# Two of the four sums of weight blocks of a pair made by accumulating transfers of GpSimd's queue

## The chip, the cores and the metric

The kernel runs on one core of a Trainium2 chip. The metric is the device time of one execution in microseconds (us). The profile names the engines PE (TensorE), DVE (VectorE), ACT (ScalarE), POOL (GpSimd) and SP (SyncE, which here issues most loads and stores).

## The reference

One inference step of a two-layer decoder of width 1024 in float32, for a prompt of 512 positions and 8 samples of 8 positions, together 576 columns. Layer 0 is a gated short convolution, layer 1 an mLSTM block with matrix memory:

```python
# layer 0
b_gate, c_gate, xa, z = split(h @ w_in, 4)          # 1024 -> 4 x 2048
conv = causal_dwconv(c_gate * xa, buf, conv_w)
out  = (b_gate * conv * silu(z)) @ w_out            # 2048 -> 1024
# layer 1
xm, z = split(h @ w_in, 2)                          # 1024 -> 2 x 2048
xc = silu(causal_dwconv(xm, conv_buf, conv_w) + conv_b)
q, k, v = xc @ w_q, xc @ w_k, xm @ w_v              # 2048 -> 2048 each
...
hh, C, n, m = mlstm_chunkwise(q, k, v, gates, C0, n0, m0)
out = ((layernorm(hh) * onorm_w) + skip * xc) * silu(z) @ w_out
```

Each layer begins with an RMS norm and ends with a residual add; a last norm follows.

## The kernel before, in words

Activations lie in SBUF as tiles of 128 channels x 576 columns. A chunk of weights is 512 KB: 128 partitions x 8 blocks of 128 x 128, that is 1024 inputs for 128 outputs. To keep float32 accuracy every product is made of three matmuls: both operands are split into a high part (cast to fp32r on ScalarE, `wh`, L250 or L202) and the rest (VectorE, `wl`, L251 or L203). There are four buffers each for `wh` and `wl`.

In 38 places two chunks are worked on as a pair, by a Strassen-like scheme (`block_pair`): the pair's weights are four blocks a11, a12 (of the tile r1) and a21, a22 (of r2), and seven products of 12 matmuls (128 x 288 columns) take the place of eight. The products, in order, are p6 with s2, p1 with a11, p5 with s1, then a12, a21, a22 and again s2. For them four sums of blocks are made on VectorE, each 128 x 512:

- s1 = a21 + a22 (L286) and s2 = s1 + a11 (L287), in `block_weights`, called ahead of the pair;
- a21 + a11, in place (L327), and s2 + a12, in place (L328), in `block_pair`, for the fifth and the seventh product.

The activations' forms (`fa`, `fb`: differences of the halves of two tiles, L257 to L260, with their `hi` and `lo`) are the other operands.

14 pairs are in layer 0 (the c_gate and xa chunks; after each pair two plain chunks for b_gate and z run into `acc`, L222), 8 make the values (v) and 16 the keys and queries of layer 1; there each pair also adds two plain chunks (L368). Layer 1's input projection (`acc`, then `xm`, L628, its short convolution `xc`, L440 and L442) runs just ahead of the value pairs. After a value or a key pair, GpSimd copies the samples' columns (`dup`, `kd`, L671), TensorE transposes them (`ta`, `tb`) and they are stored.

All loads of weights leave from SP's queue, in order. A scheduler sets the order of the instructions on each engine when the program is built, from its own model of the times; on the chip each engine works through its list strictly in order and waits on semaphores where an operand or a buffer isn't ready. So a wait at the head of a list holds all that stands behind it. `weight_tile()` gives one of a few raw weight tiles, `X(...)` a scratch tile of another small pool.

Of the kernel before, what the change touches and what calls it, by code (L numbers as in the profile page):

```python
# [12 lines left out]
ALU = mybir.AluOpType  # L13
# [54 lines left out]
def trunk(tc, io):  # L68
    nc = tc.nc
    ctx = ExitStack()  # L70
    with ctx:
# [32 lines left out]
        def X(n=NT, name="x"):  # L104

            if not layer0[0]:
                return T(n, name=name)
            uid[0] += 1
            return loads[1].tile([P, n], F32, name=f"{name}{uid[0]}", tag="X", bufs=7)
# [13 lines left out]
        def block(name="blk"):  # L123
            uid[0] += 1
            return accs[1].tile([P, 512], F32, name=f"{name}{uid[0]}", tag="blk", bufs=4)[:, 0:HT]
# [12 lines left out]
        load = nc.sync.dma_start  # L138
        store = nc.sync.dma_start
        store_act = nc.scalar.dma_start  # L140

        cols = const.tile([P, NCOL], F32, name="cols")
        cst = const.tile([P, NCST], F32, name="cst")
# [31 lines left out]
        def run(n=1):  # L175
            for _ in range(min(n, len(work))):
                work.popleft()()
# [14 lines left out]
        def weight_tile():  # L192
            return load_tile("wr", "raw").rearrange("p a (k x) -> p (a k) x", x=P)
# [51 lines left out]
        def parts_of(src):  # L245

            uid[0] += 1
            hi = wpool.tile([P, 4, P], F32R, name=f"wh{uid[0]}", tag="hi", bufs=4)
            lo = wpool.tile([P, 4, P], F32R, name=f"wl{uid[0]}", tag="lo", bufs=4)
            last_act[0] = nc.scalar.copy(hi, src).ins  # L250
            nc.vector.tensor_tensor(lo, src, hi.bitcast(F32), ALU.subtract)  # L251
            return hi, lo
# [26 lines left out]
        def block_weights(c1, c2):  # L279

            r1, r2 = weight_tile(), weight_tile()
            for r, c_ in ((r1, c1), (r2, c2)):
                latest[0] = load(out=r, in_=io["wts"][c_]).ins
            a11, a12, a21, a22 = [r[:, i:8:2, :] for r in (r1, r2) for i in range(2)]
            s1, s2 = [X(512, name="ws").rearrange("p (k x) -> p k x", x=P) for _ in range(2)]
            nc.vector.tensor_tensor(s1, a21, a22, ALU.add)  # L286
            nc.vector.tensor_tensor(s2, s1, a11, ALU.add)  # L287
            ahead_of[c1, c2] = a11, a12, a21, a22, s1, s2

        def block_pair(c1, c2, fs, xs, out1, out2, add, mid=None, then=None, pops=0):  # L290

            a11, a12, a21, a22, s1, s2 = ahead_of.pop((c1, c2))
            o11, o12, o21, o22 = out1[:, 0:HT], out1[:, HT:NT], out2[:, 0:HT], out2[:, HT:NT]
            pu = X(name="pu")
            p, u = pu[:, 0:HT], pu[:, HT:NT]
            tt = nc.vector.tensor_tensor

            def product(bank_, w, form, start):  # L300
                for j in range(4):
                    hi, lo = fs[j][form]
                    for i, (a, x) in enumerate(((w[0], hi), (w[0], lo), (w[1], hi))):
                        nc.tensor.matmul(bank_, a[:, j, :], x, start=(start and j == 0 and i == 0), stop=(j == 3 and i == 2),  # L304
                                         skip_group_check=True)

            b1 = block("p6")
            product(b1, parts_of(s2), "t2", True)
            b0 = block("p1")
            product(b0, parts_of(a11), "b11", True)  # L310
            nc.scalar.copy(p, b0)
            run(pops)
            b2 = block("p5")
            product(b2, parts_of(s1), "t1", True)
            if add:
                tt(o12, o12, b1, ALU.subtract)
                tt(o12, o12, p, ALU.add)
            else:
                tt(o12, p, b1, ALU.subtract)
            run(pops)  # L320
            product(b0, parts_of(a12), "b21", False)
            if add:
                tt(o22, o22, b2, ALU.subtract)
                tt(o22, o22, p, ALU.subtract)
            else:
                tt(o22, p, b2, ALU.add)
            tt(a21, a21, a11, ALU.add)  # L327
            tt(s2, s2, a12, ALU.add)  # L328
            run(pops)
            product(b1, parts_of(a21), "t3", False)  # L330
            run(pops)
            b3 = block("p4")
            product(b3, parts_of(a22), "t4", True)
            tt(u, b1, p, ALU.subtract)
            if add:
                tt(o22, o22, b1, ALU.add)
            else:
                tt(o22, b1, o22, ALU.subtract)
            run(pops)
            product(b2, parts_of(s2), "b22", False)  # L340
            if mid:
                mid()
            if then:
                block_weights(*then)
            if add:
                tt(o11, o11, b0, ALU.add)
                tt(o21, o21, b3, ALU.add)
                tt(o21, o21, u, ALU.add)
            elif xs is None:
                nc.scalar.copy(o11, b0)  # L350
                tt(o21, b3, u, ALU.add)
            else:
                plain(b3, b1, c2 + 1, xs, False)
                tt(o21, b3, u, ALU.add)
                tt(o22, b1, o22, ALU.add)
                plain(b0, b2, c1 + 1, xs, None)
                nc.scalar.copy(o11, b0)
            tt(o12, o12, b2, ALU.add)
# [114 lines left out]
        for k in range(KD):  # L473
# [3 lines left out]
            if k in (0, 3):  # L477
                for c_ in range(2):
                    i = 4 * (k // 3)
# [1017 lines left out]
def _chunks(w):  # L1497
    k, m = w.shape
    return w.reshape(k // D, KD, P, m // P, P).transpose(3, 0, 2, 1, 4)


def _arrays(a):
    f = {n: np.asarray(v) for n, v in a.items()}
    x = np.concatenate([f["x_prompt"].reshape(NP, D), f["x_sample"].reshape(NS, D)], 0)
    win = _chunks(f["a_w_in"][0]).reshape(4, NW, P, KD, P)
    ain = win[[1, 2, 3, 0]].transpose(1, 0, 2, 3, 4)
    bin_ = _chunks(f["b_w_in"][0])
    kq = np.stack([_chunks(f["b_w_k"][0]), _chunks(f["b_w_q"][0])], 1)
    wts = np.concatenate([t.reshape(-1, P, KD, P) for t in (
        ain, _chunks(f["a_w_out"][0]), bin_[:NW], _chunks(f["b_w_v"][0]), kq, bin_[NW:], _chunks(f["b_w_out"][0]))], 0)  # L1510
    cols = np.zeros((P, NCOL), np.float32)

    def put(name, v):
        v = v.reshape(-1, P).T
        cols[:, COLS[name]:COLS[name] + v.shape[1]] = v

    put("norm0", f["norm_w"][0])
    put("norm1", f["norm_w"][1])
    put("fin", f["final_norm_w"])
    for j in range(3):  # L1520
        put(f"ca{j}", f["a_conv_w"][0, j])
    for j in range(4):
        put(f"cb{j}", f["b_conv_w"][0, j])
    put("cbias", f["b_conv_b"][0])
    put("skip", f["b_skip"][0])
    put("onorm", f["b_onorm_w"][0])
    cols[:, COLS["eps"]] = 1e-6

    def ext(st):
        n = st.shape[1]  # L1530
        e = np.zeros((4, P, 4, 8, 8 + n), np.float32)
        e[..., :n] = st.reshape(8, n, 4, 4, P).transpose(2, 4, 3, 0, 1)
        return e.reshape(4, P, -1)

    wif = f["b_w_if"][0].reshape(3, 4, 4, P, 8)[[2, 1, 0]]
    wp = np.zeros((3, 4, P, 4, 32), np.float32)
    wp[..., :8] = wif.transpose(0, 1, 3, 2, 4)
    cst, keep, dmask = _consts()
    g16 = np.zeros((16, 42), np.float32)
    bif = f["b_b_if"][0]  # L1540
    g16[:, 0] = np.repeat(bif[:4], 4)
    g16[:, 1] = np.repeat(bif[4:], 4)
    g16[:, 2:10] = np.repeat(f["state_m"][0].T, 4, 0)
    g16[:, 10:] = dmask
    cs = f["state_C"][0].reshape(2, 4, 4, 4, P, 512).transpose(2, 0, 3, 4, 1, 5)
    ns = f["state_n"][0].reshape(2, 4, 4, 4, P).transpose(4, 2, 0, 3, 1)
    return {
        "xT": x.T.reshape(KD, P, NT), "wts": wts, "cols": cols, "cst": cst, "g16": g16, "keep": keep,
        "exa": ext(f["state_conv_a"][0]), "exb": ext(f["state_conv_b"][0]), "wif": wp.reshape(12, P, P),
        "cs": cs.reshape(32, P, 4, 512), "nst": ns.reshape(P, 128),  # L1550
    }
# [42 lines left out]
```

## Time and profile before

| | us |
|---|---|
| three runs | 1714.5, 1715.65 (median), 1722.03 |
| profiled execution, its time | 1715.56 |
| span in the profile, first to last instruction | 1713.5 |
| TensorE busy | 1669.4 (97%) |
| VectorE busy | 1105.3 (65%) |
| ScalarE busy | 685.3 (40%) |
| GpSimd busy | 107.7 (6%) |

A row of a timeline gives the start, the duration (both us), the engine, the line, the operation, out<-in, the shape, how many, and in brackets how long the engine sat idle before it and what released it. `SPq` and `ACTq` rows are issues of transfers on the queues of SP and ACT; their duration is that of the issue, and where several are put together (x2), from the first to the last. A row of waits gives the engine and operation, what it waited for, the total in us, how often, and the longest. A row of a group ends with its busy time, the mean of one in ns, and the idle time ahead of it.

In the profile the pairs of layer 0 run from 51 us to about 390 us, the value pairs from 612 us, the key/query pairs from 837 to 1271 us. After that come the matrix memory and the output projection, without pairs.

### The profile page before, as it was taken

How to read it: one execution, taken by the hardware profiler on the slowest of the kernel's cores; microseconds unless marked ns; L12 is line 12 of the kernel's file. 1: busy time of each engine (PE TensorE's matmuls, PEld its weight loads, DVE VectorE, ACT ScalarE, POOL GpSimd, SP SyncE). 2: the span in 40 equal slices, each digit the busy share in tenths (PEclk: the TensorE clock that was granted, in tenths of full speed). 3: DMA queues.
4: the chain of work that ended last, by engine and by line, in shares of the span. 5: the costliest groups of instructions: out<-in, count | busy, mean ns of one | idle time of the engine just before them, and what ended most of it. 6: DMA issues, size and time to landing. Idle time of an engine off the chain costs nothing.

```text
span 1713.5 us, 30944 instructions
## 1 busy us (share of the span) xinstructions
PE 1669.4 (97%) x12315; PEld 1591.1 (93%) x12315; DVE 1105.3 (65%) x2078; ACT 685.3 (40%) x1252; POOL 107.7 (6%) x241
## 2 busy tenths in 40 slices
PE   9999999999999999999999999999999998898998
PEld 8999999999999999999999889899899787898898
DVE  6977877774436896555846345355468556778755
ACT  5433343342323553433534233233246455554421
POOL 0000000000000001000110010000021000000000
PEclk9999999999999999999999999999999899999999
DMA  5223322223432434434423552642745588797973
GB/s 193 74 83 99 103 86 85 90 73 137 141 115 87 141 122 151 138 111 154 152 88 120 188 178 87 219 154 62 271 161 195 201 280 286 247 361 249 362 276 105
DMA packets 107487, 275.23 MB, mean 161 GB/s; under 512 B 11056, under 2 KB 33456, under 8 KB 107344
## 3 DMA queue, kind: packets, MB, share of 16 engines
q1 hardware_dynamic: 91984, 255.95, 45.0%
q10 hardware_dynamic: 15360, 17.32, 2.9%
q8 instruction: 97, 1.59, 0.4%
q14 instruction: 46, 0.38, 0.1%
HBM read 211.13 MB, written 62.09 MB: 159 GB/s over the span
## 4 chain that ended last, share of the span: by engine, by line
PE 88%; DMA 5%; DVE 4%; ACT 2%; issue 1%; SPq 0%; POOL 0%; DVEq 0%; ACTq 0%; POOLq 0%
PE acc L222 34%; PE p L304 24%; PE p L368 16%; DMA c<-cs 2%; PE qa L759 2%; PE r L1122 2%; DMA cs_out<-c 1%; DMA wr<-wts 1%; PE g L661 1%; PE num L1175 1%; PE ta L680 1%; PE cp L1175 1%; PE num L1176 1%; PE s L778 1%; PE blk L368 1%
## 5 line engine op out<-in xcount | busy, mean ns | idle before, releaser
L222 PE MATMUL acc<-hi,wh 128*128 128x256 f32 (+1 forms) x1520 | 331.7, 299 | 11.1 <-ACT z L875 6.8
L222 PE MATMUL acc<-hi,wl 128*128 128x256 f32 (+1 forms) x1520 | 330.8, 299 | 0.0
L222 PE MATMUL acc<-lo,wh 128*128 128x256 f32 (+1 forms) x1520 | 330.2, 299 | 0.0
L202 ACT CAST wh<-wr 128x512 fp32r<-128x512 f32 x286 | 176.5, 621 | 328.6 <-PE acc L222 174.5
L304 PE MATMUL p<-hi,wh 128*128 128x288 f32 x968 | 286.7, 299 | 3.7 <-ACT wh L250 2.1
L304 PE MATMUL p<-lo,wh 128*128 128x288 f32 x968 | 284.5, 295 | 0.0
L304 PE MATMUL p<-hi,wl 128*128 128x288 f32 x968 | 279.2, 295 | 1.2 <-DVE wl L251 1.2
L222 PEld LDWEIGHTS acc<-hi,wh 128*128 128x128 f32 x1520 | 257.8, 191 | 16.0 <-ACT z L875 7.0
L203 DVE TENSOR_TENSOR wl<-wr,wh 128x512 fp32r<-128x512 f32 x286 | 195.8, 689 | 118.4 <-ACT wh L202 115.8
L222 PEld LDWEIGHTS acc<-hi,wl 128*128 128x128 f32 x1520 | 257.8, 191 | 2.2 <-issue 1.2
L222 PEld LDWEIGHTS acc<-lo,wh 128*128 128x128 f32 x1520 | 257.7, 191 | 0.7 <-issue 0.5
L250 ACT CAST wh<-wr 128x512 fp32r<-128x512 f32 x152 | 94.5, 622 | 258.4 <-PE p L368 116.7
L304 PEld LDWEIGHTS p<-hi,wh 128*128 128x128 f32 x968 | 181.9, 188 | 7.8 <-ACT wh L250 3.7
L304 PEld LDWEIGHTS p<-lo,wh 128*128 128x128 f32 x968 | 182.4, 188 | 0.0
L304 PEld LDWEIGHTS p<-hi,wl 128*128 128x128 f32 x968 | 179.9, 188 | 1.4 <-DVE wl L251 1.4
L368 PE MATMUL p<-hi,wh 128*128 128x288 f32 x736 | 169.9, 299 | 0.0
L368 PE MATMUL p<-lo,wh 128*128 128x288 f32 x736 | 166.9, 294 | 0.0
L368 PE MATMUL p<-hi,wl 128*128 128x288 f32 x736 | 166.4, 296 | 0.2 <-DVE wl L203 0.2
L251 DVE TENSOR_TENSOR wl<-ws,wh 128x512 fp32r<-128x512 f32 x114 | 78.7, 691 | 119.6 <-ACT wh L250 119.4
L250 ACT CAST wh<-ws 128x512 fp32r<-128x512 f32 x114 | 70.8, 621 | 187.8 <-PE p L368 108.3
L251 DVE TENSOR_TENSOR wl<-wr,wh 128x512 fp32r<-128x512 f32 x152 | 104.9, 691 | 52.3 <-ACT wh L250 50.5
L368 PEld LDWEIGHTS p<-hi,wh 128*128 128x128 f32 x736 | 120.8, 188 | 14.7 <-issue 11.2
(371 smaller groups left out, 2557.2 us busy)
## 6 DMA issues: line engine op xcount, KB each, us to landing
wr<-wts SPq DMA_DIRECT2D x222, 512.0 KB, 3.6
c<-cs SPq DMA_DIRECT2D x112, 512.0 KB, 5.8
cs_out<-c SPq DMA_DIRECT2D x64, 512.0 KB, 6.7
x<-xT SPq DMA_DIRECT2D x16, 288.0 KB, 4.1
xcs<-xc ACTq DMA_DIRECT2D x16, 288.0 KB, 2.2
x<-xcs SPq DMA_DIRECT2D x16, 288.0 KB, 4.1
x<-x1s SPq DMA_DIRECT2D x16, 288.0 KB, 4.5
ld<-xcs SPq DMA_DIRECT2D x16, 288.0 KB, 7.5
```

The source lines that it names most:

```text
L202: last_act[0] = nc.scalar.copy(hi, raw[:, 4 * i:4 * i + 4, :]).ins
L203: nc.vector.tensor_tensor(lo, raw[:, 4 * i:4 * i + 4, :], hi.bitcast(F32), ALU.subtract)
L222: nc.tensor.matmul(acc[:, o:o + j - i], a[:, k % 4, :], x[:, i:j], start=(first and k == 0 and p == 0), stop=(last and k == 7 and p == 2))
L250: last_act[0] = nc.scalar.copy(hi, src).ins
L251: nc.vector.tensor_tensor(lo, src, hi.bitcast(F32), ALU.subtract)
L304: nc.tensor.matmul(bank_, a[:, j, :], x, start=(start and j == 0 and i == 0), stop=(j == 3 and i == 2), skip_group_check=True)
L368: nc.tensor.matmul(b, a[:, k % 4, :], x[:, t:t + HT], start=bool(new) and k == 0 and i == 0, stop=(k == 7 and i == 2), skip_group_check=True)
L661: nc.tensor.matmul(g[32 * j:32 * j + 32, 0:b - a], w[:, 32 * j:32 * j + 32], tiles[j][:, a:b], start=True, stop=True)
L680: nc.tensor.transpose(pa[:, 128 * it:128 * it + 128], t[:, 128 * it:128 * it + 128], ident)
L759: nc.tensor.matmul(st["q"][32 * g:32 * g + 32, :], st["qp"][dt // 2][:, dt % 2, 128 * u + 32 * g:128 * u + 32 * g + 32], ct[g // 2][:, g % ...
L1122: nc.tensor.matmul(r, kst[2 * i + j][:, 128 * dt:128 * dt + 128], vst[:, 0:512], start=True, stop=True)
L1175: nc.tensor.matmul(acc[:, 256:512], w, b[:, 0:256], **ends)
```

## The change

s1 and a21 + a11 are no longer made by VectorE. The host lays the blocks of the chunks concerned out so that the blocks of the even inputs come first (a permutation of the eight blocks; a11 is then `r1[:, 0:4]`, a12 `r1[:, 4:8]`). s1's tile is loaded with the first half of chunk c2 from HBM (256 KB, SP), and a transfer of GpSimd's queue with `accum_op` add then adds c2's second half to it. Another such transfer adds c1's first half to a21 in the tile r2. s2 and its second sum stay on VectorE. Line numbers behind move by one to three (L287 becomes L290, L251 becomes L252, L628 L630, L671 L673).

```diff
+        add_load = nc.gpsimd.dma_start
...
             for r, c_ in ((r1, c1), (r2, c2)):
                 latest[0] = load(out=r, in_=io["wts"][c_]).ins
-            a11, a12, a21, a22 = [r[:, i:8:2, :] for r in (r1, r2) for i in range(2)]
+            a11, a12, a21, a22 = [r[:, i:i + 4, :] for r in (r1, r2) for i in (0, 4)]
             s1, s2 = [X(512, name="ws").rearrange("p (k x) -> p k x", x=P) for _ in range(2)]
-            nc.vector.tensor_tensor(s1, a21, a22, ALU.add)
+            load(out=s1, in_=io["wts"][c2][:, 0:4, :])
+            add_load(out=s1, in_=io["wts"][c2][:, 4:8, :], accum_op=ALU.add)
+            add_load(out=a21, in_=io["wts"][c1][:, 0:4, :], accum_op=ALU.add)
             nc.vector.tensor_tensor(s2, s1, a11, ALU.add)
...
-            tt(a21, a21, a11, ALU.add)
             tt(s2, s2, a12, ALU.add)
...
+    blk = [c for c in range(8, 64) if c % 4 < 2] + list(range(96, 192, 2))
+    wts[blk] = wts[blk][:, :, [0, 2, 4, 6, 1, 3, 5, 7]]
```

In the whole program VectorE has 76 instructions fewer, SP 38 loads more, GpSimd 76 transfers more. TensorE's list keeps its instructions and nearly their order. Three places show what else moved.

The first pair of layer 0, on VectorE. The rows give line, operation, out<-in, shape; `wr_644` and `wr_645` are r1 and r2, `ws_648` is s1, `ws_649` s2. Before:

```order
L286 TENSOR_TENSOR ws_648<-wr_645 128x512
L258 TENSOR_TENSOR fa_654<-x_133,fa_654 128x288
L287 TENSOR_TENSOR ws_649<-ws_648,wr_644 128x512
L327 TENSOR_TENSOR wr_645<-wr_645,wr_644 128x4x128
L260 TENSOR_TENSOR fb_655<-x_133,fa_654 128x288
L160 TENSOR_TENSOR lo_661<-fa_654,hi_660 128x576
L251 TENSOR_TENSOR wl_702<-ws_649,wh_701 128x512
```

And now:

```order
L161 TENSOR_TENSOR lo_663<-fa_656,hi_662 128x576
L161 TENSOR_TENSOR lo_667<-fb_657,hi_666 128x576
L544 TENSOR_TENSOR u_504<-raw_306,raw_304 128x576
L439 COPY ext_502<-u_504 128x8x8
L581 TENSOR_TENSOR z_684<-raw_379,rb_464 128x576
L290 TENSOR_TENSOR ws_649<-ws_648,wr_644 128x512
L442 SCALAR_TENSOR_TENSOR cv_505<-u_504,cols,cv_505 128x511
L444 SCALAR_TENSOR_TENSOR cv_505<-ext_502,cols,cv_505 128x64
L442 SCALAR_TENSOR_TENSOR cv_505<-u_504,cols,cv_505 128x510
L252 TENSOR_TENSOR wl_704<-ws_649,wh_703 128x512
```

The s2 sum stands behind the last two `fa` and `fb`, both `lo`, and `u`, `ext` and `z` of the convolution, which came behind the pair's `wl` rows before; on ScalarE the activations `cv` and `z` likewise stand ahead of the cast of s2.

The first value pair, on VectorE and GpSimd. Before, on VectorE (`ws_6840` is s1, `ws_6841` s2):

```order
L286 TENSOR_TENSOR ws_6840<-wr_6837 128x512
L440 SCALAR_TENSOR_TENSOR xc_6823<-xm_6333,cols,xc_6823 128x511
L442 SCALAR_TENSOR_TENSOR xc_6823<-ext_6056,cols,xc_6823 128x64
L287 TENSOR_TENSOR ws_6841<-ws_6840,wr_6836 128x512
L327 TENSOR_TENSOR wr_6837<-wr_6837,wr_6836 128x4x128
```

Now, first on VectorE, then on GpSimd (`ws_6854` is this pair's s1, `ws_6855` its s2; `wr_7161` is r2 of the second pair, `ws_7164` its s1):

```order
L290 TENSOR_TENSOR ws_6855<-ws_6854,wr_6850 128x512
L630 TENSOR_TENSOR xm_6919<-acc_6860,rb_5883 128x576
L439 COPY ext_6693<-xm_6919 128x8x8
L252 TENSOR_TENSOR wl_7040<-ws_6855,wh_7039 128x512
L252 TENSOR_TENSOR wl_7057<-wr_6850,wh_7056 128x512
L330 TENSOR_TENSOR ws_6855<-ws_6855,wr_6850 128x512
L252 TENSOR_TENSOR wl_7075<-ws_6854,wh_7074 128x512
L161 TENSOR_TENSOR lo_6922<-xm_6919,hi_6921 128x576
L630 TENSOR_TENSOR xm_6996<-acc_6937,rb_5883 128x576
```

```order
L289 DMA wr_7161<-wts 128x512
L288 DMA ws_6854<-wts 128x512
L640 COPY cpb<-xm_6919 128x3
L640 COPY cpb<-xm_6996 128x3
L288 DMA ws_7164<-wts 128x512
```

The s2 sum now has the `xm` of the last two input chunks behind it, and on GpSimd the transfer that makes s1 stands behind the second pair's a21. On SP the load into `ws_6854` (L287) stands right behind the loads of the second pair, `wr_7160` and `wr_7161`.

The first two key/query pairs, on SP. Before, with `wr_9859` and `wr_9860` the second pair's r1 and r2:

```order
L283 DMA wr_9859<-wts 128x1024
L283 DMA wr_9860<-wts 128x1024
L171 DMA x_9373<-xcs 128x576
L171 DMA x_9375<-xcs 128x576
```

And now, with `ws_9424` s1 of the first pair, `ws_9886` that of the second, `wr_10034` r1 of the third:

```order
L284 DMA wr_9882<-wts 128x1024
L284 DMA wr_9883<-wts 128x1024
L172 DMA x_9395<-xcs 128x576
L172 DMA x_9397<-xcs 128x576
L287 DMA ws_9424<-wts 128x512
L689 DMA vss_7026<-tb_9461 256x1x128
L689 DMA vss_7026<-tb_9487 256x1x128
L689 DMA vss_7026<-tb_9624 256x1x128
L689 DMA vss_7026<-tb_9650 256x1x128
L284 DMA wr_10034<-wts 128x1024
L287 DMA ws_9886<-wts 128x512
```

The loads into s1 stand behind the last `x` loads and behind the third pair's r1. In the steady rows of layer 0 the load of s1 stands between r1 and r2 of the same pair.

## The prediction

> **What bounds the kernel now.** I read the page from the top: busy shares, chain, costliest groups; then DVE's groups by line, the busy time by stage, and PE's waits in the stages with pairs.
>
> ```profile
> span 1713.5 us, 30944 instructions
> PE 1669.4 (97%) x12315; PEld 1591.1 (93%) x12315; DVE 1105.3 (65%) x2078; ACT 685.3 (40%) x1252; POOL 107.7 (6%) x241
> PE 88%; DMA 5%; DVE 4%; ACT 2%; issue 1%; SPq 0%; POOL 0%; DVEq 0%; ACTq 0%; POOLq 0%
> ...
> L286 DVE TENSOR_TENSOR ws<-wr 128x512 f32<-128x512 f32 x38 | 26.1, 688 | 0.3
> L327 DVE TENSOR_TENSOR wr<-wr,wr 128x512 f32<-128x512 f32 x38 | 26.1, 686 | 0.0
> ```
>
> TensorE is busy 97% of the span and carries 88% of the chain, VectorE 4%. The two kinds of sum that leave VectorE are the last two rows: 52.2 us of its 1105.3. What that is worth is read where TensorE idles (columns of the first four rows: stretch, its length, busy time of each engine, then clock, DMA share, GB/s):
>
> ```profile
> 40.00:880.00 840.00, 830.61 (x6269) 823.89 (x6269) 581.20 (x1072) 332.42 (x566) 42.77 (x81) 1.00 0.36 112
> 80.00:320.00 240.00, 240.00 (x1809) 240.00 (x1808) 186.31 (x336) 95.29 (x163) 5.86 (x10) 1.00 0.30 93
> 600.00:640.00 40.00, 37.71 (x277) 36.65 (x276) 39.68 (x84) 21.91 (x35) 2.74 (x2) 1.00 0.39 123
> 880.00:1280.00 400.00, 398.95 (x3004) 366.23 (x3003) 201.68 (x362) 129.92 (x229) 40.55 (x106) 1.00 0.46 154
> ...
> PE p L304 <- ACT wh L250: 2.1, 1, 2.1
> PE p L304 <- DVE wl L251: 1.2, 1, 1.2
> PE tb L682 <- POOL dup L671: 1.1, 1, 1.1
> ```
>
> From 80 to 320 us and from 880 to 1280 us, where most of the 38 pairs run, TensorE loses 0 and 1.05 us: there a shorter VectorE can give nothing. Only from 600 to 640 us is VectorE full (39.68 of 40) while TensorE loses 2.29 us. So the question is not what the 76 removed instructions cost, but whether the sums, made by another road, are still there in time.
>
> **The new road and its price.** T is the time from GpSimd's issue of an accumulating transfer to its landing. The trace of before has none, nor any other transfer issued by GpSimd, so T is bounded by the nearest rows (columns: size, median us to landing):
>
> ```profile
> xcs<-xc ACTq DMA_DIRECT2D x16, 288.0 KB, 2.2
> wr<-wts SPq DMA_DIRECT2D x222, 512.0 KB, 3.6
> ld<-xcs SPq DMA_DIRECT2D x16, 288.0 KB, 7.5
> wr<-wts SPq DMA_DIRECT2D x4, 256.0 KB, 5.6
> ```
>
> Below: 2.2 us, the fastest of about this size. Above: 11.2 us, twice the 256 KB load of the same weights into the same kind of tile, as if destination and source were fetched one after the other. I take 5.6 us, that load itself: same bytes, same two memories, the accumulate taken as free; the four of them were issued among others at the start, which makes it dear, and the added read makes up for that. A plain load of 256 KB I take at 3.6 us, the median of the 512 KB ones. The Trainium skill, page "DMA: Bandwidth & Descriptors", section "Anatomy of one DMA — SWDGE (gpsimd) path", fits a transfer issued from GpSimd by 2.0 us plus its bytes over 436 GB/s; for 256 KB that is an estimate of 2.6 us, it says nothing there of accumulating, and the sum below would be +2.6 us instead of +7.7. No run here shows it yet.
>
> **The change, part by part.** Removed: 76 VectorE instructions, 52.2 us. They lie beside a busy TensorE nearly everywhere; what they can give back is TensorE's 1.2 us wait for `wl`, which VectorE made late. I take −1.2 us; the ends are 0 and −2.3 us, all that TensorE loses from 600 to 640 us.
>
> Added: 38 loads on SP, 76 transfers on GpSimd, 114 × 256 KB = 30 MB beside the 275 MB moved. DMA share in the rows of the pair stages is 0.30 to 0.46, so I cost the bytes at nothing; that cover would go where the engines are nearly full, which none of these rows shows. The sum s1 is the one that counts: VectorE still adds s2 = s1 + a11, ScalarE casts s2, and the first product of a pair (p6) needs that cast. In VectorE's order whatever stands behind that add waits for s1 too.
>
> *First pair of layer 0.* Here T hardly matters, the order does.
>
> ```profile
> 36.63 0.43 SPq L536 DMA_DIRECT2D ext<-exa  x1
> 48.48 0.45 DVE L259 TENSOR_TENSOR fb<-x,x 128x288 f32<-128x288 f32 x1
> 49.81 0.68 DVE L287 TENSOR_TENSOR ws<-ws,wr 128x512 f32<-128x512 f32 x1
> 49.93 0.67 ACT L159 CAST hi<-fa 128x576 fp32r<-128x576 f32 x1
> 50.59 0.62 ACT L250 CAST wh<-ws 128x512 fp32r<-128x512 f32 x1
> 51.26 0.40 PE L304 MATMUL p<-hi,wh 128*128 128x288 f32 x1 [2.07 <-ACT wh L250]
> ```
>
> TensorE already waits 2.07 us here for the cast of s2. The new order puts two `fa`/`fb`, two `lo` (L161), `u`, `ext` and `z` ahead of the s2 add on VectorE, and the two activations `cv` and `z` ahead of the cast on ScalarE. From 48.84 us: two `fa`/`fb` at 0.36 apart; `lo` when the cast of `fa` is done (about 50.5), then 0.66 each for `lo`, `lo`, `u`, 0.1 for `ext`, 0.66 for `z`: the s2 add at about 53.2 instead of 49.81, done 53.9, cast behind ScalarE's `z` at about 54.0, TensorE at 54.6. That is +3.3 us. Ends: 0, if `lo` and `z` found slack I don't see, and +4 us. s1 itself: load issued at 37.1, landed 40.7, plus 5.6: long there.
>
> *First value pair.*
>
> ```profile
> 593.32 6.66 SPq L283 DMA_DIRECT2D wr<-wts  x2
> 602.09 0.69 DVE L287 TENSOR_TENSOR ws<-ws,wr 128x512 f32<-128x512 f32 x1
> 605.41 0.75 DVE L628 TENSOR_TENSOR xm<-acc,rb 128x576 f32<-128x576 f32 x1
> 611.06 0.76 DVE L628 TENSOR_TENSOR xm<-acc,rb 128x576 f32<-128x576 f32 x1 [0.32 <-PE acc L222]
> 611.96 0.38 PE L304 MATMUL p<-hi,wh 128*128 128x288 f32 x1 [0.94 <-DVE xm L628]
> ```
>
> The two loads of 593.32 are the second pair's r1 and r2; the second leaves at 599.65, and in the new order the first pair's s1 load comes only behind it, at 600.0, landing 603.6. On GpSimd the second pair's a21 transfer, which needs that r2 (603.3), stands ahead of the s1 transfer: s1 leaves at about 604.5 (1 us for the one ahead, an estimate) and lands at 604.5 + T. Behind the s2 add then stand an `xm`, an `ext`, two `wl`, the sum L330, another `wl`, a `lo`, and only then the `xm` that frees TensorE's bank: 0.6 + 0.66 + 0.1 + 4 × 0.6 + 0.66 = 4.5 us of starts, and 0.9 from that `xm` to TensorE, as in the last two rows. TensorE at 609.9 + T instead of 611.96: a loss of T − 2.1, here +3.5 us (0.1 and 9.1 at the ends).
>
> *First two key/query pairs.*
>
> ```profile
> 823.88 0.91 SPq L171 DMA_DIRECT2D x<-xcs  x2
> 833.01 0.69 DVE L287 TENSOR_TENSOR ws<-ws,wr 128x512 f32<-128x512 f32 x1
> 837.09 0.40 PE L304 MATMUL p<-hi,wh 128*128 128x288 f32 x1 [0.72 <-ACT k L382]
> 839.60 2.55 SPq L283 DMA_DIRECT2D wr<-wts  x2
> 843.65 0.63 ACT L250 CAST wh<-ws 128x512 fp32r<-128x512 f32 x1 [1.00 <-PE p L304]
> 848.32 0.29 PE L304 MATMUL p<-hi,wh 128*128 128x288 f32 x1
> ```
>
> The first pair's s1 load stands behind the two `x` loads: issued 824.8, landed 828.4, s1 at 834.0 against the 833.01 at which the s2 add began: +1.0. The second pair's s1 load stands behind the next pair's r1, which leaves at 839.60: issued 839.9, landed 843.5, s1 at 843.5 + T, 1.3 us more for the s2 add and the cast, against 848.32: T − 3.5, which contains the +1.0 before it. Both together +2.1 us (0 and 7.7).
>
> *All other pairs.*
>
> ```profile
> 150.29 3.77 SPq L283 DMA_DIRECT2D wr<-wts  x2
> 160.14 0.68 DVE L287 TENSOR_TENSOR ws<-ws,wr 128x512 f32<-128x512 f32 x1
> 166.42 0.76 DVE L579 TENSOR_TENSOR z<-acc,rb 128x576 f32<-128x576 f32 x1 [1.05 <-PE acc L222]
> 898.24 3.65 SPq L208 DMA_DIRECT2D wr<-wts  x2
> 921.22 0.29 PE L304 MATMUL p<-hi,wh 128*128 128x288 f32 x1
> ```
>
> Layer 0: s1's load goes between r1 (150.29) and r2, lands at 154.2, its sum at 159.8, just ahead of the old s2 add (160.14). A `wl` for TensorE's second chunk stands 1.3 us behind that add; TensorE wants it at about 166.4, when the first chunk ends (the `z` row). So the sum may come up to 164.4: T up to 10. Key/query pairs: load issued 901.9, landed 905.5, sum at 911.1, TensorE at 921.22: nothing either, up to about T = 10. The sum a21 costs nothing anywhere: its transfer leaves when r2 is there, and the fifth of seven products needs it, 4 × 1.6 us behind p6 (seven take 848.32 − 837.09 = 11.2 us). What hides s1 in the 34 other pairs is this lead of 4 us or more; were it gone, s1 would be late in every period.
>
> On SP the s1 loads are 0.33 us each; behind the one at 600.0 stands a chunk load that left at 612.92 before, so nobody waits for it. On GpSimd the copies `dup`, `kd`, `cpa` stand behind transfers that wait for landings; that engine is busy 6% and TensorE waited for it once, 1.1 us.
>
> The sum, with T from 3.5 to 10: 3.3 + (T − 2.1) + (T − 3.5) − 1.2 = 2T − 3.5. At 5.6 us it is +7.7 us. The profiled run took 1715.56 us (span 1713.5 and 2.06 around it), next to the median of 1715.65: 1723.3 us.
>
> **The rivals.** *Faster:* the late sums don't bite and VectorE's relief frees TensorE's stalls. From 40 to 880 us TensorE idles 9.4 us in all, 2.07 of it at 51.26. To be faster by over 0.5% (8.6 us, about what a measurement of this kernel can tell from no change) all of that must vanish; it decides only if the first pair's s2 add comes no later than before and T is below 2.1 us. It would end at about 1707. Against it: the new order at 48.84 us, which has the s2 add behind seven others.
>
> *Quick transfers:* T between 2 and 3.5 us. Key/query pairs lose nothing, the value pair 0 to 1.4: +2 to +3.5 us, 1718 to 1719. For it: the 2.2 us row.
>
> *Middling transfers:* T from 6 to 10 us gives +8.6 to +16.5 us, 1724 to 1732. For it: 256 KB at 5.6 us without any adding.
>
> *Slow transfers:* T over 10 us. Then s1 is late in each of 13 layer-0 periods by T − 10.2. At 11.2: first pair 4.0, value pair 9.1, key/query 7.7, periods 13 × 1.0, less 1.2: +32.6 us, 1748; at 13 us it is past 1770. Against it: no row of this size is above 7.5 us.
>
> *GpSimd in order:* transfers that wait hold up `dup`, on which TensorE's transposes of values and keys depend. 24 pairs with some 0.5 us each, half of the 1.1 us wait, would add 12 us: 1735. Against it: GpSimd's long idle time.
>
> **How the numbers follow.** T from 3.5 to 6 us, my forecast (1719 to 1724): 0.30. Quick: 0.20. Middling: 0.28. Slow: 0.13. GpSimd's order: 0.05. Faster: 0.04. Up to T = 6 the loss stays within 0.5%: same 0.50, slower 0.46, faster 0.04. The range runs from 1716, which leaves out the faster rival and little more, to 1748, T at its upper end; what lies beyond is some 0.15.
>
> **What would show it.** VectorE's busy time falls by about 52 us and TensorE's does not. In the DMA list the accumulates appear with their T. TensorE's wait at the first p6 of layer 0 grows from 2.07 to about 5.4 us and names the cast of s2; new waits of 2 to 4 us stand at the first value pair and the second key/query pair; from 80 to 320 us it stays full. The prediction is wrong if T is over 10 us, if TensorE loses time in every period, or if `dup` becomes what it waits for.

## The result, and the profile after

| | before | changed |
|---|---|---|
| median of 6 runs each, us | 1718.22 | 1728.98 |
| lowest and highest, us | 1714.5, 1722.03 | 1726.72, 1730.06 |
| span of the profiled execution, us | 1713.5 | 1726.7 |

The changed kernel takes 1.0061 times as long, 95% interval 1.0047 to 1.0076. When it was run once more beside before, the ratio was 1.0069 (1.0047 to 1.0091). It is slower by 10 to 12 us; the forecast was 1723.3 us, +7.7.

The page of the changed kernel: span, busy time, queues, and the transfers that were added.

```profile
span 1726.7 us, 31144 instructions
PE 1669.4 (97%) x12315; PEld 1592.0 (92%) x12315; DVE 1063.0 (62%) x2002; ACT 683.2 (40%) x1252; POOL 169.2 (10%) x317
...
q1 hardware_dynamic: 97456, 265.91, 46.4%
q0 software_dynamic: 10944, 19.93, 7.4%
...
wr<-wts POOLq DMA_DIRECT2D x38, 256.0 KB, 4.2
ws<-wts SPq DMA_DIRECT2D x38, 256.0 KB, 3.9
ws<-wts POOLq DMA_DIRECT2D x38, 256.0 KB, 4.5
```

TensorE is busy for the same 1669.4 us (1667.7 in a second profile), so by this count what was lost is idle time; the matmuls that a lower clock slowed, below, are some 2 us and don't stand out in it. VectorE is busy 42.3 us less, not 52.2: the rows of single instructions overlap their neighbours (0.69 us each at starts 0.60 apart), and the busy time counts an overlap once. Without the 76 rows, the busy time of before would be 40.5 us less. The accumulating transfers have a queue of their own, q0. They land 4.2 and 4.5 us after their issue: that is T.

TensorE's waits in the changed kernel (what waited, for what, total, times, longest):

```profile
PE p L307 <- ACT wh L251: 6.8, 2, 5.6
PE qa L761 <- DMA c<-cs: 6.6, 7, 1.6
PE p L307 <- DVE xm L630: 5.0, 1, 5.0
...
PE p L307 <- DVE wl L252: 1.2, 2, 0.9
```

They were 2.1, 1.1, 0.9 and 1.2 us. To place the loss I compare the start of the same TensorE instruction in the two traces; the table gives what each stretch added, by before's time.

| stretch, us of before | forecast | changed kernel | the same, second profile |
|---|---|---|---|
| first pair of layer 0, to 58 | +3.3 | +3.7 | +3.5 |
| rest of layer 0 and input chunks, to 600 | 0 | 0.0 | 0.0 |
| first value pair, 600 to 633 | +3.5 | +6.0 | +6.1 |
| 633 to 660 (forecast: VectorE's relief) | −1.2 | −1.5 | −1.3 |
| 660 to 820 | 0 | −0.8 | −0.7 |
| first key/query pairs, 820 to 858 | +2.1 | +2.7 | +2.7 |
| 858 to 1055 | 0 | −0.3 | −0.3 |
| **sum at 1055** | **+7.7** | **+9.9** | **+10.0** |
| 1055 to 1231 | 0 | +5.9 | +2.7 |
| behind the pairs | 0 | −2.5 | −2.1 |

Up to 1055 us the two profiles agree to 0.3 us in every line; from there on an execution varies by some us.

The first pair of layer 0, a timeline of the changed kernel:

```profile
53.59 0.69 DVE L290 TENSOR_TENSOR ws<-ws,wr 128x512 f32<-128x512 f32 x1
54.36 0.62 ACT L251 CAST wh<-ws 128x512 fp32r<-128x512 f32 x1
55.03 0.61 PE L307 MATMUL p<-hi,wh 128*128 128x288 f32 x1 [5.63 <-ACT wh L251]
```

VectorE's s2 add starts at 53.59 without any wait for s1 (49.81 before; the hand count gave 53.2), and TensorE at 55.03 (51.26; the count gave 54.6). The first value pair, in the same view:

```profile
603.82 0.40 SPq L287 DMA_DIRECT2D ws<-wts  x1
608.30 0.86 POOL L289 DMA_DIRECT2D wr<-wts  x1 [4.88 <-issue]
609.57 0.88 POOL L288 DMA_DIRECT2D ws<-wts  x1 [0.41 <-issue]
614.26 0.69 DVE L290 TENSOR_TENSOR ws<-ws,wr 128x512 f32<-128x512 f32 x1 [7.22 <-DMA ws<-wts]
618.85 0.75 DVE L630 TENSOR_TENSOR xm<-acc,rb 128x576 f32<-128x576 f32 x1
619.74 0.58 PE L307 MATMUL p<-hi,wh 128*128 128x288 f32 x1 [4.97 <-DVE xm L630]
620.12 0.44 PE L307 MATMUL p<-lo,wh 128*128 128x288 f32 x1
```

From the load of s1's first half to s1's landing it took 10.4 us (forecast 10.1); from the s2 add to the `xm` that frees the bank 4.6 us (4.5); from there 0.9 (0.9). VectorE stood still for 7.22 us with that `xm` behind the add. The last two rows show something else: the matmuls take 0.44 us and start 0.24 us apart. The granted clock in short stretches (the first two columns are the stretch and its length, the clock stands third from the end), changed kernel first, before's first value pair last:

```profile
606.00:612.00 6.00, 6.00 (x47) 6.00 (x47) 1.04 (x3) 0.78 (x1) 1.75 (x2) 1.00 0.69 168
619.00:623.00 4.00, 3.26 (x14) 3.29 (x14) 4.00 (x9) 1.55 (x3) 0.58 (x1) 0.50 0.25 53
623.00:627.00 4.00, 4.00 (x24) 4.00 (x24) 3.62 (x9) 1.84 (x4) 0.67 (x1) 0.72 0.52 199
627.00:631.00 4.00, 4.00 (x32) 4.00 (x31) 2.88 (x7) 2.64 (x5) 0.21 (x1) 1.00 0.74 142
```

```profile
612.00:616.00 4.00, 4.00 (x30) 4.00 (x31) 4.00 (x9) 3.27 (x6) 0.46 (x1) 1.00 0.48 95
```

Behind the wait of 4.97 us TensorE was granted half its clock and did 24 matmuls in a busy 4 us (623 to 627) where it does 32 at full clock.

### The profile page after: what moved, and what is told of

It is laid out like the page before. It is cut to its first block, busy times and chain, and to the rows that moved or that the text cites. A ratio compares the mean times of both kernels' runs of the same rounds, so it can differ in the third digit from the quotient of the medians.

```text
span 1726.7 us, 31144 instructions
## 1 busy us (share of the span) xinstructions
PE 1669.4 (97%) x12315; PEld 1592.0 (92%) x12315; DVE 1063.0 (62%) x2002; ACT 683.2 (40%) x1252; POOL 169.2 (10%) x317
## 3 DMA queue, kind: packets, MB, share of 16 engines
q0 software_dynamic: 10944, 19.93, 7.4%
## 4 chain that ended last, share of the span: by engine, by line
PE 82%; DMA 9%; DVE 5%; ACT 2%; issue 2%; SPq 1%; ACTq 0%; POOL 0%; DVEq 0%; POOLq 0%
PE acc L223 33%; PE p L307 22%; PE p L370 14%; DMA c<-cs 4%; DMA wr<-wts 2%; DMA ws<-wts 2%; PE qa L761 2%; PE r L1124 1%; PE cp L1177 1%; PE cp L1178 1%; PE num L1177 1%; PE num L1178 1%; PE s L780 1%; DVE xc L442 1%; PE ta L682 1%
## 5 line engine op out<-in xcount | busy, mean ns | idle before, releaser
L223 PE MATMUL acc<-hi,wh 128*128 128x256 f32 (+1 forms) x1520 | 330.9, 299 | 10.8 <-ACT z L877 6.8
L251 ACT CAST wh<-wr 128x512 fp32r<-128x512 f32 x152 | 94.3, 620 | 238.2 <-PE p L370 92.2
L251 ACT CAST wh<-ws 128x512 fp32r<-128x512 f32 x114 | 70.7, 620 | 188.7 <-PE p L370 73.2
L252 DVE TENSOR_TENSOR wl<-wr,wh 128x512 fp32r<-128x512 f32 x152 | 104.7, 689 | 51.7 <-ACT wh L251 48.1
L252 DVE TENSOR_TENSOR wl<-ws,wh 128x512 fp32r<-128x512 f32 x114 | 78.6, 690 | 76.9 <-ACT wh L251 75.2
```

The source lines that it names most:

```text
L223: nc.tensor.matmul(acc[:, o:o + j - i], a[:, k % 4, :], x[:, i:j], start=(first and k == 0 and p == 0), stop=(last and k == 7 and p == 2))
```

## The experiments

Twelve kernels. Where one was run several times, the ratio to before with its interval is given; where once, only its trace. Their line numbers differ by a few from those above.

**Layout alone.**

```diff
-            load(out=s1, ...); add_load(out=s1, ...); add_load(out=a21, ...)
+            nc.vector.tensor_tensor(s1, a21, a22, ALU.add)     # and a21 += a11 in block_pair
```

> All four sums back on VectorE, the weights still laid out by block. Theory (the loss comes from s1 being late and from the added transfers): span within 1.5 us of the 1713.5 of before, TensorE's wait at the first pair back to about 2.1 us, no wait at the first value pair beyond 0.9 us. Rival (the layout, or the operands' form, costs something): the sums on VectorE take another time than 0.69 us, or the span is 3 us or more above before.

Ratio 0.9994 (0.9978 to 1.0009), span 1713.6; TensorE waits 2.1 us at the first pair and 0.9 at the first value pair. The other layout costs nothing; what was lost came with the transfers. The trace holds a warning for the table above. TensorE, VectorE, ScalarE and GpSimd work through the same lists as before, and all four sums are on VectorE; still TensorE gained 1.5 us from 633 to 660 us and lost 0.7 from 820 to 858. The wait for `wl` stayed at 1.2 us; the one for GpSimd's copies `dup` (1.1 us in before) is gone, since the same four copies took less time. First before, then this kernel:

```profile
642.44 5.07 POOL L671 COPY dup<-v 128x128 f32<-128x128 f32 x4 [29.98 <-DVE v L358]
```

```profile
642.36 2.16 POOL L680 COPY dup<-v 128x128 f32<-128x128 f32 x4 [29.98 <-DVE v L367]
```

Why the copies differ, no run shows. So a difference of some 1.5 us in a stretch proves nothing about the edit, unless a wait that the edit touches is seen to change.

**Only a21 + a11 by transfer.**

```diff
-            load(out=s1, in_=...); add_load(out=s1, ...)
+            nc.vector.tensor_tensor(s1, a21, a22, ALU.add)
             add_load(out=a21, in_=io["wts"][c1][:, 0:4, :], accum_op=ALU.add)
```

> Only the sum a21 + a11 by the accumulating transfer, s1 on VectorE: 38 transfers, no added loads. Theory (late s1 is the first half of the loss, the DMA time of the added transfers under the state loads c the second): no loss at the first pair (0 instead of +3.3 us), at the first value pair (0 instead of +5.6) and at the first key/query pairs (0 instead of +2); between 1100 and 1230 us a loss of 1 to 3 us, since a little under half of the added DMA time is left; span 1713 to 1717. Rival (GpSimd's queue as such delays the kernel): losses at those places stay at half or more, span 1719 or more.

No loss at any of the places (TensorE's waits 2.1 and 0.9 us again), and none from 1100 to 1230 us: TensorE was 3.0 us ahead of before at 1231 us. So GpSimd's queue as such delays next to nothing (TensorE waits 2.6 us for `dup` instead of 1.1); it is the late s1. The span was all the same 1720.5 and the ratio 1.0042 (1.0024 to 1.0060), against what I expected: behind 1340 us this kernel lost some 10 us. Of the last 2697 instructions of TensorE, which stand behind the pairs, 505 are others than before's in the same place, while in the changed kernel none is; the kernel with 37 transfers, below, tests it.

**Key/query pairs back on VectorE.**

```diff
-            load(out=s1, ...) ...                    # every pair
+            if c1 < 128: load(out=s1, ...) ...       # layer 0 and values; else the sums on VectorE
```

> Key/query pairs with all sums on VectorE, layer-0 and value pairs by transfers. Theory (the loss from 1100 to 1230 us is contention of the state loads c with the added transfers): that stage loses less than 1 us, first pair still +3.3, first value pair still +5.6, a gain of 1.6 behind it, span about 1720 to 1721. Rival (that loss is carried over from the earlier ones, or comes with a lower clock): the stage still loses 4 us or more, span 1725 or more.

Span 1717.0, ratio 1.0029 (1.0015 to 1.0044). First pair +3.0, first value pair +6.3, −1.0 behind it; from 820 to 858 us 0.0, from 858 to 1055 +0.2, from 1055 to 1231 +0.2. Waits of TensorE up to 1300 us:

```profile
PE p L312 <- ACT wh L251: 5.6, 1, 5.6
PE p L312 <- DVE xm L637: 5.3, 1, 5.3
PE qa L768 <- DMA c<-cs: 0.7, 2, 0.5
```

The loss from 820 to 858 us goes with the transfers of that stage. The one from 1055 to 1231 us is gone as well, but a second profile, below, shows that one execution says little there. (The span fell further than the two places say; behind the pairs it varies, and the median of ten runs was 1722.5 us.)

**The same transfers without adding.**

```diff
-            add_load(out=s1, in_=io["wts"][c2][:, 4:8, :], accum_op=ALU.add)
-            add_load(out=a21, in_=io["wts"][c1][:, 0:4, :], accum_op=ALU.add)
+            add_load(out=s1, in_=io["wts"][c2][:, 4:8, :])
+            add_load(out=a21, in_=io["wts"][c1][:, 0:4, :])
```

> The same 76 transfers of GpSimd's queue without the adding (they overwrite, so the two sums are left out of the result). Theory A (the adding costs DMA time: destination read as well): issue to landing falls from 4.5 to about 3.5 us, the DMA share from 80 to 320 us from 0.48 to about 0.40, the loss between 1100 and 1230 us from 5.5 to 2 to 4 us; first pair unchanged at +3.3, since it is order; span 1720 to 1724. Theory B (what costs is the road over GpSimd, not the adding): landing, share and span as with adding, 1726 or so.

Ratio 1.0007 (0.9994 to 1.0019), span 1717.8. The page:

```profile
q0 software_dynamic: 6080, 19.93, 3.8%
...
wr<-wts POOLq DMA_DIRECT2D x38, 256.0 KB, 3.0
...
ws<-wts POOLq DMA_DIRECT2D x38, 256.0 KB, 3.3
```

Theory A: the adding makes 144 packets of a transfer instead of 80, doubles its DMA time (7.4% to 3.8% of 16 engines for the same 19.93 MB), and adds 1.2 us to its landing. The DMA share from 80 to 320 us fell from 0.48 to 0.40, as expected. First pair +4.2, no better than with adding, since nobody waits for s1 there; first value pair +2.1 instead of +6.0, though T fell by only 1.2; first key/query pairs +0.6 instead of +2.7; nothing lost from 1055 to 1231 us, where 2 to 4 were expected. Its rows, wait and clock:

```profile
618.46 0.37 PE L312 MATMUL p<-hi,wh 128*128 128x288 f32 x1 [3.29 <-DVE xm L637]
...
620.00:624.00 4.00, 4.00 (x33) 4.00 (x32) 4.00 (x9) 1.73 (x4) 0.00 (x0) 1.00 0.82 240
```

The wait is 3.29 us instead of 4.97, and the clock stays at 1.00.

**The four pairs that start a stage on VectorE.**

```diff
-            load(out=s1, ...) ...
+            if c1 not in (8, 96, 128, 132): load(out=s1, ...) ...     # else the sums on VectorE
```

> The four pairs that start a stage (first of layer 0, first of the values, first two of keys and queries) make all their sums on VectorE again; the other 34 keep the transfers. Theory: the losses at 55 us (+3.3), 613 us (+5.6) and 835 to 848 us (+2) go to 0 to 0.5 each, the gain of about 1.5 us behind the first value pair stays, the loss from 1100 to 1230 us stays at 4 to 6 us since the transfers there stay; span about 1716 to 1719. Rival (the late sum only moves on to the next pair of the stage, which then leads it): the losses come back within two pairs, span 1722 or more.

First pair +0.2, first value pair −0.5 (wait 0.94), TensorE 1.7 us ahead at 820 us. Ratio 1.0027 (1.0012 to 1.0041). These two places are mended, and the loss does not come back with the next pair of layer 0 or of the values. From 820 to 858 us there remain +3.5, against what I expected, because the edit misses its target there. The kernel takes the heads in the order 3, 0, 1, 2, so the first two key/query pairs have c1 = 176 and 180, and 128 and 132 are the fifth and sixth. In the trace the sum s1 is made on VectorE at 48.6, 600.9, 904.1 and 928.4 us; the first key/query pair still waits for its transfer:

```profile
832.63 0.69 DVE L295 TENSOR_TENSOR ws<-ws,wr 128x512 f32<-128x512 f32 x1 [1.46 <-DMA ws<-wts]
```

On VectorE the copies of a transpose (`tb`) stand behind this add, and TensorE waits 1.94 us for them, then 0.56 for the second pair's cast. So this run tests the key/query stage not at all; for that stage there is the kernel with its sums back on VectorE, above. From 1055 to 1231 us the loss was 1.2, expected 4 to 6.

**a21 alone, in 37 pairs; and in the 24 value and key/query pairs.**

```diff
+            if c1 != 8:  add_load(out=a21, ..., accum_op=ALU.add)     # first kernel
+            if c1 >= 96: add_load(out=a21, ..., accum_op=ALU.add)     # second kernel
```

> Only the sum a21 + a11 by the transfer, and not in the first pair of layer 0: 37 transfers. Against the kernel with 38 of them the list of TensorE behind the pairs is another one: 44 instead of 213 of its rows stand elsewhere than before. Theory (that kernel's loss behind 1360 us, 10 us, came from the order of the instructions there and not from the transfers): the 3 us that it had gained at 1223 us are there again and the stage behind loses less than 3 us; span 1710 to 1714. Rival (the transfers leave something behind, in buffers or in the clock): a loss of 6 us or more behind 1360 us, span 1717 or more.

> The sum a21 + a11 by the transfer in the 24 value and key/query pairs alone, layer 0 all on VectorE. Theory: what VectorE gives back lies only from 600 us on, so this keeps the whole gain: -1.4 us at 640 us, -0.6 at 835 us, some -1 by 1223 us; span 1710 to 1714, as the kernel with 37 transfers. Rival (gain comes from layer 0 too): 1 us or more less gain than that kernel.

The first: 1710.26 against 1715.88 us, ratio 0.9972 (0.9957 to 0.9988), TensorE 2.9 us ahead at 1231 and 6.1 at the end. The second: 1711.42, ratio 0.9975 (0.9962 to 0.9987); its profiled execution was its slowest (1716.79). Both beat both kernels, by little. Leaving one transfer out of the kernel with 38 of them turned 1.0042 into 0.9972; both are 3 us ahead at 1231 us, so the difference lies behind the pairs, where no transfer runs and the order is another (161 instructions of TensorE instead of 505 differ from before's in their place; the expectation counts otherwise). That the order alone makes it is the likely reading and not shown: TensorE's last 2697 instructions took 433.3 us in the kernel with 38 transfers and 420.2 here, but also from 420.4 to 429.8 in seven profiles of kernels that keep before's order there, before's own among them. Within the pairs, before's wait of 1.2 us for `wl` is gone in both (−1.1 and −1.0 from 633 to 660 us): that is VectorE's relief, put at −1.2 in the forecast. The rest of the gain I can't assign.

**The changed kernel again; s1 alone; a21's transfer three times.**

```diff
+            # s1 alone: a21 + a11 on VectorE, s1 as in the changed kernel
+            # three times: as the kernel with 37 transfers, and for c1 >= 128
+            for _ in range(2):
+                add_load(out=a21, in_=io["wts"][c1][:, 0:4, :], accum_op=ALU.add)
```

> The changed kernel once more, unaltered, for a second profile. If the loss between 1055 and 1230 us (TensorE waiting for the states c) is a property of the program: 4 to 6 us again there, and 3.3 / 5.6 / -1.5 / 2 at the earlier places to 0.3 us. If it is chance of one execution: it differs by 2 us or more while the earlier places repeat.

Repeated up to 1055 us; from 1055 to 1231 us +2.7 instead of +5.9, TensorE's wait for c 2.7 instead of 6.6. So more than half of that loss was chance of one execution.

> Only s1 by load and accumulating transfer; a21 + a11 on VectorE. Theory: the first pair of layer 0 loses 3.3 us as before (order of VectorE's list); at the first value pair no second pair's a21 stands ahead on GpSimd, so s1's transfer leaves when its load has landed, 1.3 us earlier or more: a loss of 3.5 to 4.5 instead of 5.6 us. Rival (the late s1 there is set by the load behind the second pair's r2 alone): 5.6 us again.

At the first value pair s1's transfer left as its load had landed and TensorE waited 4.11 us instead of 4.97:

```profile
602.25 0.42 SPq L289 DMA_DIRECT2D ws<-wts  x1
607.74 0.93 POOL L290 DMA_DIRECT2D ws<-wts  x1 [5.89 <-DMA ws<-wts]
617.32 0.58 PE L312 MATMUL p<-hi,wh 128*128 128x288 f32 x1 [4.11 <-DVE xm L637]
...
617.00:621.00 4.00, 3.68 (x15) 3.71 (x16) 4.00 (x10) 1.97 (x3) 0.64 (x1) 0.50 0.34 60
```

From load to transfer 5.5 us, not 5.75: the second pair's a21 ahead on GpSimd cost little, the load behind r2 nearly all. The stretch lost 5.5 us (expected 3.5 to 4.5), since the clock falls here as well. The first pair of layer 0 lost 3.3 us from 50 to 55 us, as expected.

> As the kernel with 37 transfers for a21 alone, but each of the 16 key/query pairs issues its transfer three times (a11 is added three times, so this part of the result is another). s1 stays on VectorE, so no sum that is wanted early is late. Theory (contention: the transfers' DMA time delays the states c): the DMA share between 1100 and 1130 us rises from 0.71 to 0.85 or more and TensorE loses 3 us or more between 1055 and 1230 us against the kernel with single transfers, waiting for c. Rival (that stage's loss in the changed kernel comes from the s1 chain): less than 1 us.

The DMA share from 1100 to 1130 us rose to 0.89, but from 1055 to 1231 us TensorE lost 1.7 us, 0.7 more than with single transfers (1.0). The theory of contention, as I had put a number on it, fell. (From 820 to 858 us this kernel lost 10 us: three chained transfers, 4 to 5 us each, made even a21 late for its product.) TensorE's wait for c was 1.1 us in before, 0.6 to 2.0 in five kernels without s1 transfers in the key/query pairs (2.8 with the tripled ones), 1.7 to 6.6 in seven profiles with them. So it tends to be longer with them, by some 2 us; how, stays open.

**TensorE kept busy through the wait.**

```diff
+        b = mm("warm")           # behind the last input chunk
+        for _ in range(30):
+            nc.tensor.matmul(b[:, 0:256], warm[:, 0:128], warm, start=True, stop=True)
```

> The changed kernel with 30 matmuls on a tile of zeros (result unused) between the last input chunk and the first value pair, in the time in which TensorE waits there for s1. Theory (the wait of 5 us lowers the granted clock to 0.5 for some 5 us, which costs about 2.4 us beside the wait): clock 1.00 over the first products of the value pair, p6 starts where it did (+9.0 to +9.4 us in all), but the 0.9 us that came at 617 us and about 1.5 of the 5.6 us are gone: +7.5 to +8 us behind the first value pair instead of +10. Rival (the clock is given by something else, or the first products are slow for want of operands): +10 us again there.

Timeline and clock:

```profile
616.02 3.44 PE L663 MATMUL warm<-warm 128*128 128x256 bf16 x30 [1.18 <-DVE xm L637]
620.08 0.37 PE L312 MATMUL p<-hi,wh 128*128 128x288 f32 x1 [0.63 <-DVE xm L637]
620.42 0.29 PE L312 MATMUL p<-hi,wl 128*128 128x288 f32 x1
...
623.00:627.00 4.00, 4.00 (x31) 3.87 (x30) 4.00 (x10) 2.36 (x5) 0.43 (x1) 1.00 0.57 213
```

p6 starts where it did, 8.1 us behind before (7.8 in the changed kernel), but the clock is 1.00 and the products behind run 0.13 us apart: from p6 to 633 us this kernel loses nothing (−0.3 us), the changed one 2.0. The clock is what made the first products slow. Half of it went again at once, since TensorE, faster now, waits for VectorE (`wl`, 1.1 us just behind 633 and then 0.6). The kernel as a whole was no faster (span 1728.9): it lost 4.3 us from 820 to 858 and 3.0 from there to 1055, for which I have no reason.

**The first value pair's weights asked for six chunks earlier.**

```diff
-            if f == NW - 3:
+            if f == NW - 9:
                 block_weights(96, 98)
```

> The changed kernel with the weights of the first value pair asked for six input chunks earlier, so that the load of s1 leaves SP ahead of the loads of the second pair; TensorE's list behind the pairs is that of before. Theory (the loss at 613 us is the late s1 alone, 4.1 us of wait and 2.4 us of clock): that loss goes to 0 to 0.5 us, all else stays; about 6 us less than the changed kernel at 1055 us (+3.5 to +4.5 instead of +10.1). Rival (in VectorE's list something else is late there, or r1 and r2, taken early, hold weight tiles that the input chunks want): 3 us or more remain between 560 and 620 us.

The rival won: ratio 1.0061 (1.0037 to 1.0084). The wait at 613 us is back at 0.9, but the s2 add now stands earlier in VectorE's list and there waits 2.75 us for s1 as well (at 577.65 us); an input chunk's `xm` behind it is late (+3.9 us by 600 us), and the second value pair, whose s2 add waits 4.28 us at 635.69, is late in its place (+2.7 from 633 to 660). Of the 3.8 us in the first row, 1.6 were there before:

```profile
PE acc L223 <- DVE xm L637: 3.8, 2, 2.2
...
PE p L312 <- DVE v L363: 3.2, 1, 3.2
```

## Why the prediction was right, and where its terms were off

The time lay in the range. Forecast was +7.7 us, just within 0.5%; measured +10.8, just beyond. T itself, 4.5 us against 5.6, was the better for the kernel; by 2T − 3.5 it would have been +5.5. So T, taken too large, made up for part of what the other terms lack, and that +7.7 came so near is in part luck. The measured 1729 us falls among the times of the rival with middling transfers, whose condition, T from 6 to 10 us, was not met. (By the formula that rival starts at +8.5 us, not at +8.6.) Step by step:

- *TensorE is the bound, so VectorE's relief is worth next to nothing*: right in size, for 42 us of VectorE; but that −1.3 to −1.5 us behind the first value pair met the forecast's −1.2 is luck. The wait for `wl` that was to go is still there, 1.2 us, now in two parts; what went is the wait for `dup`, and it went with the layout alone as well (−1.5), with all sums on VectorE. Only with a21 alone did the wait for `wl` go (−1.0 to −1.1). The −0.8 up to 820 us came in one step at 782 us, where TensorE waits for nothing; I can't assign it.
- *First pair of layer 0, order and not T*: right, +3.5 and +3.7 against +3.3, +4.2 with faster transfers, +0.2 with the sums on VectorE.
- *First value pair, T − 2.1*: the chain was right and came out at 10.4 us from load to sum. Of its terms T was too large by 1.0 and the landings ahead of it too small: r2's load took 4.9 us to its transfer's issue, not 3.6. The step that was missing is what a wait of this length does next: at 0.50 of the clock the products behind it lost another 2 us. TensorE was 4.0 us later at p6, and 6.0 at 633 us. That is the term that was mis-sized: +6.0 instead of +3.5.
- *First two key/query pairs, T − 3.5 together*: +2.7 against +2.1, and 0.0 with all key/query sums on VectorE. By T = 4.5 the formula says +1.0. The first pair's s2 add waited 1.06 us for s1, and TensorE behind it 1.8 for the copies `tb`, 0.8 later in all (the formula had +1.0); the second's transfer left 4.5 us after its load, not 3.6, and the pair added 1.9.
- *All other pairs hidden*: right up to 1055 us (0.0 from 58 to 600, −0.3 from 858 to 1055). Not foreseen: the longer waits for c behind it, +5.9 and +2.7 us.
- *DMA bytes at nothing*: right for layer 0, where the share rose from 0.30 to 0.48 and TensorE lost nothing:

```profile
80.00:320.00 240.00, 240.00 (x1809) 240.00 (x1808) 171.94 (x310) 94.20 (x161) 23.19 (x30) 1.00 0.48 125
```

- *The rivals*: GpSimd's order fell with the kernel of a21 alone (TensorE waits 2.6 us for `dup` there instead of 1.1, and is ahead of before all the same). The faster one was kept off by the first pair, as its condition said.

The 2.6 us, an estimate worked out from the fit on the Trainium skill's page "DMA: Bandwidth & Descriptors" ("Anatomy of one DMA — SWDGE (gpsimd) path"), stand against 3.0 and 3.3 us without adding, issued and landed beside other loads, and 4.2 and 4.5 with it: the adding, 1.2 us here, is not in the fit.

On the clock, the Trainium skill's page "TensorE: Matmul & The Clock Gate", section "Part 1: The HAM clock gate (the "warmup" mystery)", says that TensorE goes to half clock after an idle window of some 3.4 us and that the windows run freely. The traces agree on the window: in all 14 the granted clock changes at steps of 3.41 us. The waits of 4.11 and 4.97 us (0.50) each held a whole idle step; that of 3.29 us (1.00) did not. But a whole idle step is more than it takes, and here the measurement decides. Before's wait of 2.07 us lay in one step, and the next had half the clock; the wait of 3.29 us without adding was shared by two steps, each of them busy for 1.77 us (columns as above: stretch, length, TensorE's busy time, clock third from the end; before first):

```profile
48.13:51.55 3.42, 1.35 (x10) 1.11 (x9) 3.42 (x9) 2.26 (x4) 0.00 (x0) 1.00 0.00 0
51.55:54.96 3.41, 3.41 (x15) 3.17 (x15) 3.41 (x6) 1.79 (x4) 0.00 (x0) 0.50 0.02 5
```

```profile
613.40:616.82 3.42, 1.77 (x14) 1.53 (x12) 3.39 (x7) 3.06 (x6) 0.21 (x1) 1.00 0.00 0
616.82:620.23 3.41, 1.77 (x13) 1.80 (x14) 3.41 (x8) 1.73 (x3) 0.58 (x1) 1.00 0.04 7
```

In the 14 traces TensorE was busy for less than 0.45 of a step at full clock 73 times, and each time the next step had half the clock. From 0.45 to 0.72 it went both ways. Above 0.72 the clock fell behind 18 of 6240 steps, all between 1337 and 1391 us; why there, no run shows.

## What to carry to other kernels

When the engine that is relieved is not the bound, look only at what the new road delays: an operand that comes later stalls everything behind its first reader on an in-order engine, and asking for it earlier can, as here, only move that reader up in the list, where it waits all the same. A wait that leaves TensorE busy for less than about half of a step of 3.41 us costs more than its length, by the clock: a further 2 us behind the one of 4.97 us here. It should be priced so; a shorter wait may or may not cost it, by where it falls in the steps. Where one of two sums is wanted late and the other early, move the late one alone (0.9972 here, some 5 us, though only 1.1 of them are seen to come from the edit), and compare the order of the whole program, since a scheduler may change a stage that the edit does not touch by more than the edit is worth.

## What the runs showed of the hardware that was not expected

An accumulating transfer of 256 KB took twice the DMA time of the same transfer without adding (7.4% against 3.8% of the engines' span for 19.93 MB), 144 packets instead of 80, and 1.2 us more to land (4.2 and 4.5 us against 3.0 and 3.3). GpSimd is busy 0.87 us for the issue of each. TensorE's granted clock changes in steps of 3.41 us, and a step that is busy for less than 0.45 is enough for half the clock in the next (73 of 73); in the changed kernel half the clock lasted two steps behind the wait of 4.97 us, from 618.4 to 625.2 us.
